# Reordering the loads of an attention stage: which wait the loads of one cycle stand behind

## The chip, the cores and the metric

The kernel runs on one core of a Trainium2 chip, as one program. The time is the device time of one execution in microseconds (us); the median of several executions counts. One further execution is taken by the hardware profiler, and its trace is read in the profile: engine by engine, instruction by instruction. TensorE (PE, with its weight loads PEld) does the matmuls, VectorE (DVE) and ScalarE (ACT) work on the results, GpSimd (POOL) helps, and SyncE (SP) issues nearly all DMA transfers, strictly in the order of its own list of instructions.

## The reference

One layer of a hybrid encoder, with 2048 tokens on a grid of 32 x 64, 1024 channels and 16 heads of 64: RMS norm, one projection into queries, keys, values and gates, neighbourhood attention in two dimensions, a SiLU gate, the output projection with the residual, and a final RMS norm.

```python
h = rmsnorm(x, g)
q, k, v, gate = jnp.split(h @ w_in, 4, axis=-1)
# each query sees 8 rows x 16 columns of keys around it, with a learned bias per head and offset
s = jnp.where(col_valid, einsum(qr, kr) * scale + bias, NEG_INF)
o = einsum(softmax(s), vr)
x = x + (o * jax.nn.silu(gate)) @ w_out
return rmsnorm(x, norm_f)
```

## The kernel before

Everything is computed in float32 accuracy; large products run as three products of halves of the mantissa, with a split of each operand into a high and a low part (ScalarE copies, VectorE subtracts).

`stage_one` (L617) and `stage_two` (L1011) compute most of the projections, by a seven-product scheme, and write queries, keys, gates and values to DRAM (`qd`, `kd`, `sgd`, `vd`). Then comes the attention stage, which this change is about: the loop at L1825 to L1880 with 32 cycles and one more to end it. A cycle is one pair of heads `p` and one quarter `T` of the tokens, in the order of `order` (L1221). In program order cycle `m` is:

- `begin(m)` (L1804): makes a list of loads, which the clock then issues;
- `feed(...)`: matmuls of 512 columns that fill the time, from the projections that are still missing (`projections`, L1197) and later from the output product of the first rows (`outputs`, L1564); between them VectorE, ScalarE and GpSimd normalise the scores of the cycle before;
- `turns(m - 1)` (L1358): 48 transposes of the normalised scores, with copies by ScalarE and VectorE (L1376, L1378);
- `scores(2m)`, `scores(2m + 1)` (L1310): 64 matmuls of queries and keys, then bias and exponent (L1332, L1340);
- `values(m - 1)` (L1382): 36 matmuls of scores and values, and one product with the gate (L1399). The result, attention's output, is stored to DRAM by `keep` (L1402).

So on TensorE a cycle of about 9 us is: filling matmuls, transposes, scores, values, and again.

The order of the work is laid out by a planner that runs when the program is built. `clock[0]` counts the filling matmuls, and `now()` (L273) adds 26 for each cycle that is over. `store(key, lag, f)` (L330) puts an action into the list `later`, due `lag` matmuls from now, and `due` (L336) carries it out when the clock gets there; `later_loads` (L1796) does so for a list of loads, 0.5 apart. `all_loads` (L1800) issues those that are left when the next cycle begins.

What cycle `m` loads by `begin`, in this order: the gate of cycle m - 1 (`load_sg`, L1260), the two bias tables of cycle m + 1 (`load_bias`, L1268), its queries (`load_q`, L1243) and keys (`load_k`, L1226), and the values of cycle m (`load_v`, L1252). All are issued by SyncE. A load waits until the buffer that it overwrites is free. There are two buffers for queries, so the queries of cycle m + 1 wait for the scores of cycle m - 1 (the last before `begin(m)`); two for values, so those of cycle m wait for `values(m - 2)`. Gates have two buffers, tables ten, keys one for even and one for odd pairs of heads; these are free early. Because SyncE keeps its order, whatever stands behind the queries in the list waits for the same scores, and whatever stands behind the values waits for the values section. Keys of `T` = 0 and 3 add only four rows (128 KB) to those of the quarter before.

The second kind of loads: weight blocks. `items` (L261) lists what the fillers still need: blocks of `w_in`, four blocks of x, blocks of `w_out`. `load_ahead` (L293) keeps five of them loaded ahead of their use, and `load_item` (L154) issues the load at once, at the place of the program where the planner happens to be. `consume` (L300) uses the next block, which means the split by ScalarE and VectorE (L185, L186, L190, L191). In the attention stage it does so only in a `turn`, or when a product can't go on without it (`asked`), and only when the block was asked for at least 36 units of `now()` ago.

Of the kernel before, what the change touches and what calls it, by code (L numbers as in the profile page):

```python
# [61 lines left out]
def build(ctx, tc, x, xr, xt, wg, bias, w_out, n0, nf, out):  # L62
# [87 lines left out]
    raws, wh, wl, asked_at = {}, {}, {}, {}  # L150
# [3 lines left out]
    def load_item(it):  # L154
        kind, a, b = it
        t = raws[it] = raw([128, 512], F32, "raw")
        asked_at[it] = now()
        if kind == "x":
            nc.sync.dma_start(t, xt[a * 128:(a + 1) * 128, b * 512:(b + 1) * 512])
        elif kind == "w":  # L160
            nc.sync.dma_start(t, wg[a[0], :, 512 * b:512 * b + 512])
        else:
            nc.sync.dma_start(t, w_out[a * 128:(a + 1) * 128, b * 512:(b + 1) * 512])

    def use_item(it):
        kind, a, b = it
        state["event"] = clock[0]
        t = raws.pop(it)
        if kind == "x":
            normed("x%d1" % (a // 4 + 1), b, a % 4, t)  # L170
            split_to(hh[a, b], hl[a, b], t, None)
        elif kind == "w":
            u, ph = a
            if KINDS["v"] <= u < KINDS["g"]:
                t = t.rearrange("p (k c) -> p k c", c=256)
                a = u // 2 * 2, ph
                if u % 2 == 0:
                    wh[a, b] = wp([128, 2, 512], F32R, "wh")
                    wl[a, b] = wp([128, 2, 512], F32R, "wl")
                s = slice(u % 2 * 256, u % 2 * 256 + 256)  # L180
                h, l = wh[a, b][:, :, s], wl[a, b][:, :, s]
            else:
                w = wp([128, 2, 512], F32R, "w")
                wh[a, b], wl[a, b] = h, l = w[:, 0], w[:, 1]
            nc.scalar.activation(h, t, AF.Copy)  # L185
            nc.vector.tensor_tensor(l, t, h.bitcast(F32), OP.subtract)  # L186
        else:
            h, l = xs([128, 512], F32R, "woh"), xs([128, 512], F32R, "wol")
            woh[a, b], wol[a, b] = h, l
            nc.scalar.activation(h, t, AF.Copy)  # L190
            nc.vector.tensor_tensor(l, t, h.bitcast(F32), OP.subtract)  # L191
# [62 lines left out]
    attending = [False]  # L254
# [6 lines left out]
    items, seen = [], set()  # L261
# [11 lines left out]
    def now():  # L273
        return clock[0] + 26 * runs[0]

    freed = set()
    state = dict(used=0, loaded=0, half=-1, done_halves=0, event=0.0)

    def may_use(it):
        kind, a, b = it  # L280
        d = state["done_halves"]
        if kind == "w":
            def tiles_(a, b):
                return (a[0] // 2 * 2, a[1], b) if KINDS["v"] <= a[0] < KINDS["g"] else (*a, b)
            live = {tiles_(*i[1:]) for i in items[:state["used"]] if i[0] == "w" and last_use["w", i[1]] >= d} - freed
            return sum(1 + (KINDS["v"] <= t[0] < KINDS["g"]) for t in live | {tiles_(a, b)}) <= 8
        if kind == "x":
            return sum(last_use["x", i] >= d for i in {i[2] for i in items[:state["used"]] if i[0] == "x"} - {b}) < 2
        if kind == "o":
            return last_use["x", 2 + b] < d  # L290
        return True

    def load_ahead():  # L293
        while state["loaded"] < min(len(items), state["used"] + AHEAD):
            load_item(items[state["loaded"]])
            state["loaded"] += 1

    quiet = [False]

    def consume(n, asked=False, turn=False):  # L300
        for _ in range(n):
            load_ahead()
            if attending[0] and not asked and not turn:
                return
            if state["used"] == len(items) or not may_use(items[state["used"]]):
                return
            if attending[0] and now() - asked_at[items[state["used"]]] < 36 and not asked:
                return
            it = items[state["used"]]
            state["used"] += 1  # L310
            use_item(it)

    def need(it):
        while it in items[state["used"]:]:
            before = state["used"]
            consume(1, True)
            assert state["used"] > before, (it, items[state["used"]])
# [25 lines left out]
    def must(*keys):  # L343
        assert all(k in written for k in keys), keys
        for n in range(len(later) - 1, -1, -1):
            if later[n][1] in keys:
                for _ in range(n + 1):
                    later.pop(0)[2]()
                break
# [871 lines left out]
    order = [(p, T) for p in range(NP) for T in (1, 0)] + [(p, T) for p in range(NP - 2) for T in (2, 3)]  # L1221
# [4 lines left out]
    def load_k(p, T):  # L1226
        r0, r1, more = PARTS[T]
        base = 12 * (T > 1)
        a, b = r0 * GW, r1 * GW + more
        must(*[("k", p, c) for c in range(a // 512, (b + 511) // 512)])  # L1230

        def keys():
            if T in (1, 2):
                khalf.clear()
                KT[p, T // 2] = (kp([128, 2048], F32, "kt") if p % 2 == 0 else mkp([128, 1536], F32, "kt"))[:, :1344]
            t = KT[p, T // 2]
            if T == 2:
                nc.gpsimd.memset(t[:, 1280:1288], 0.0)
            nc.sync.dma_start(t[:, a - base * GW:b - base * GW], kd[p][:, a:b])

        return keys

    def load_q(p, T):  # L1243
        must(("q", p, T))

        def queries():
            QT[p, T] = qp([128, 512], F32, "q")
            nc.sync.dma_start(QT[p, T], qd[p][T])

        return queries  # L1250

    def load_v(p, T):  # L1252
        r0, r1 = FRAME[T], FRAME[T] + TALL
        must(*[("v", p // 4, t) for t in range(r0 // 2, (r1 + 1) // 2)])
        rows = vd[p // 4][p % 4][r0 * 8192:r1 * 8192].rearrange("(k x) -> k x", x=1024)
        t = vp([128, 1024], F32, "vt")
        VT[p, T] = t.rearrange("p (s d) -> p s d", s=8)
        nc.sync.dma_start(t[:8 * TALL], rows)

    def load_sg(p, T):  # L1260
        must(("g", p, T))
        SG[p, T] = sp([128, 512], F32, "sgt")
        nc.sync.dma_start(SG[p, T], sgd[p][T])
# [4 lines left out]
    def load_bias(p, T):  # L1268
        fs = []
        kind = BRINGS[T]  # L1270
        w = 2 * WIDE * TABLES[kind][2]
        EM[p, T // 2, kind] = []
        for quad in range(2):
            t = mp([128, 512], F32, "em")[:, :w]
            EM[p, T // 2, kind].append([t[:, :w // 2], t[:, w // 2:]])
            o = TABLE_AT[kind] + quad * w
            fs.append(lambda t=t, o=o, w=w: nc.sync.dma_start(t, bias[p, 128 * o:128 * (o + w)].rearrange("(q c) -> q c", c=w)))
        return fs
# [372 lines left out]
    def load_rows_of(m, f, home=None):  # L1651
        n, half = PAIRS[m][int(f[1]) - 1], int(f[2]) - 1
        T, i = divmod(n, 4)
        must(*[("og", p, T) for p in range(NP) if p // 4 == half])
        A[m, f] = (home or raw)([128, 512], F32, "raw")
        nc.sync.dma_start(A[m, f].rearrange("p (k q) -> p k q", k=4), ogd[T][i, half])
# [139 lines left out]
    def later_loads(fs, lag, step):  # L1796
        for k, f in enumerate(fs):
            store(("load",), lag + k * step, f)

    def all_loads():  # L1800
        while any(e[1][0] == "load" for e in later):
            later.pop(0)[2]()

    def begin(m):  # L1804
        all_loads()
        quiet[0] = False
        fs = [lambda: load_sg(*order[m - 1])] if m else []
        if m + 1 < cycles:
            nx = order[m + 1]
            fs += load_bias(*nx)  # L1810
            fs += [load_q(*nx), load_k(*nx)]
        if m < cycles:
            fs.append(lambda: load_v(*order[m]))
        later_loads(fs, 0.5, 0.5)
        if m == cycles - 1:
            later_loads([land_first], 1.5, 0)
            later_loads([lambda f=f, i=i: load_rows_of(i, f) for i in ((2, 0, 1) if PLAIN <= 6 else (0, 1)) for f in ("A11", "A12")], 10, 0.5)
        if m == cycles:
            later_loads([land_rest], 4, 0)
# [5 lines left out]
    for m in range(cycles + 1):  # L1825
        a = amount[m] - 8
        begin(m)
        feed(HALF_HEAD)
        if m:
# [88 lines left out]
```

## Time and profile before

| | |
|---|---|
| median of 3 runs | 993.05 us (992.84 to 994.57) |
| the profiled execution | 993.25 us, of which the span from first to last instruction is 991.5 us |
| granted TensorE clock | 0.999 |
| TensorE busy | 979.3 us, 99% of the span |
| VectorE, ScalarE, GpSimd busy | 76%, 54%, 16% |
| attention stage | about 560 to 870 us of the span |
| DMA in the span | 227.93 MB, mean 230 GB/s |

In the profile, L12 is line 12 of the kernel. A group of matmuls is written as its line, its output and inputs by the program's names, shapes and count. "Idle before" is time in which the engine had nothing running; behind the arrow stands what ended it, and "issue" means that the profile shows no semaphore, so no engine and no transfer, on which it waited. A matmul's end is modelled: matmuls overlap, and a short stop hides in part behind the modelled end of the matmul before. In the attention stage `q`, `kt`, `vt`, `sgt` and `em` are the loads of queries, keys, values, gate and tables, `ogd` the store of attention's output, and `raw` a weight block. A DMA's row in the timeline shows when SyncE issued it and how long issuing took; the time to landing is counted from the start of the issue.

### The profile page before, as it was taken

Reading aid. Unit: us, or ns where it says so; the run is one execution under the profiler, and the core shown is the slowest. Engines: PE = TensorE matmul, PEld = TensorE weight load, DVE = VectorE, ACT = ScalarE, POOL = GpSimd, SP = SyncE. Lnnn points to the kernel's source line nnn. Section 1 sums busy time; section 2 is a strip of 40 time slices with the busy share of each in tenths; the row PEclk is TensorE's granted clock in tenths of the full one; section 3 lists DMA queues with packets and bytes.
Section 4 is the critical chain, followed back from the end, with each engine's and each line's share of the span. In section 5 each row is a group of like instructions: output and inputs, shape, how many; then the busy total and the mean of one; then the engine's idle time right before and its main releaser. Section 6 shows DMA issues by size and latency. Waiting matters only on the chain.

```text
span 991.5 us, 22624 instructions
## 1 busy us (share of the span) xinstructions
PE 979.3 (99%) x8172; PEld 797.0 (80%) x8172; DVE 755.2 (76%) x1735; ACT 531.5 (54%) x1310; POOL 159.6 (16%) x430
## 2 busy tenths in 40 slices
PE   9999999999999999999999999999999999999997
PEld 7888888888888888888888778777778777888886
DVE  6899888988665876766775677668778878877866
ACT  7773245455535342343433467677777776654443
POOL 0000001231100000000001133333343332302110
PEclk9999999999999999999999999999999999999999
DMA  8943547777957836657565799878989978697754
GB/s 287 337 130 102 196 132 256 248 242 251 368 159 225 276 116 201 189 182 224 169 176 203 247 302 271 264 226 279 307 277 288 298 222 266 223 379 212 205 146 117
DMA packets 149968, 227.93 MB, mean 230 GB/s; under 512 B 13536, under 2 KB 66016, under 8 KB 149856
## 3 DMA queue, kind: packets, MB, share of 16 engines
q1 hardware_dynamic: 146832, 221.37, 70.2%
q0 software_dynamic: 2592, 4.72, 2.8%
q8 instruction: 64, 1.05, 0.4%
q14 instruction: 48, 0.39, 0.1%
q10 hardware_dynamic: 432, 0.40, 0.1%
HBM read 160.37 MB, written 66.06 MB: 228 GB/s over the span
## 4 chain that ended last, share of the span: by engine, by line
PE 99%; issue 1%; DVE 0%; ACT 0%
PE pp L446 40%; PE pv L612 13%; PE py L1695 12%; PE o L1395 8%; PE s L1323 6%; PE ph L1372 5%; PE pp L388 2%; PE pp L384 2%; PE pp L386 2%; PE pv L727 2%; PE po L1600 2%; PE po L1604 2%; PE po L1602 2%; PE zp L127 0%; PE prb L235 0%
## 5 line engine op out<-in xcount | busy, mean ns | idle before, releaser
L446 PE MATMUL pp<-h,f 128*128 128x512 f32 x576 | 185.3, 389 | 0.0
L446 PE MATMUL pp<-t,f 128*128 128x512 f32 x702 | 171.4, 389 | 0.0
L446 PEld LDWEIGHTS pp<-t,f 128*128 128x128 f32 x702 | 131.8, 188 | 27.4
L1340 ACT ACTIVATE x<-sums,st 128x264 f32<-128x264 f32 (+1 forms) x256 | 124.5, 488 | 30.0 <-DVE st L1332 30.0
L446 PEld LDWEIGHTS pp<-h,f 128*128 128x128 f32 x576 | 108.1, 188 | 22.6
L446 PE MATMUL pp<-l,f 128*128 128x512 f32 x288 | 112.0, 389 | 0.0
L1352 POOL TENSOR_SCALAR x<-x,st 128x264 f32<-128x264 f32 (+1 forms) x192 | 88.5, 477 | 113.7 <-DVE st L1347 93.8
L1332 DVE CUSTOM_DVE_ANT_0 sums<-s,em 128x253 f32<-128x253 f32 (+1 forms) x256 | 91.1, 401 | 6.2 <-ACT x L1340 1.7
L429 DVE TENSOR_TENSOR f<-raw,f 128x512 fp32r<-128x512 f32 x105 | 75.9, 727 | 19.4 <-ACT f L428 19.3
L1395 PE MATMUL o<-pta,vt 120*64 120x192 f32 (+2 forms) x1152 | 85.1, 300 | 4.0 <-issue 4.0
L1395 PEld LDWEIGHTS o<-pta,vt 120*64 120x64 f32 x1152 | 70.2, 137 | 23.2 <-issue 16.4
L428 ACT ACTIVATE f<-raw 128x512 fp32r<-128x512 f32 x105 | 63.4, 622 | 36.6 <-DVE raw L435 22.0
L1376 DVE COPY pta<-ph 120x512 f32<-120x512 f32 x96 | 60.3, 684 | 18.3 <-PE ph L1372 18.1
L1378 ACT ACTIVATE pta<-ph 120x512 f32<-120x512 f32 x96 | 50.4, 599 | 37.8 <-PE ph L1372 37.8
L446 PEld LDWEIGHTS pp<-l,f 128*128 128x128 f32 x288 | 54.0, 188 | 11.3
L1323 PE MATMUL s<-kt,q 64*32 64x253 f32 (+1 forms) x2048 | 59.2, 362 | 0.7 <-issue 0.7
L1372 PEld LDWEIGHTS ph<-ident,x 64*120 64x120 f32 x1536 | 47.6, 135 | 11.3 <-issue 10.6
L612 PE MATMUL pv<-wh,t 128*128 128x512 f32 x176 | 56.2, 389 | 0.0
L1695 PE MATMUL py<-woh,f 128*128 128x512 f32 x168 | 55.4, 390 | 0.0
L467 POOL TENSOR_TENSOR tmp<-tmp,rb 128x512 f32<-128x512 f32 x18 | 28.5, 1582 | 157.6 <-DVE tmp L464 137.2
L446 PE MATMUL pp<-sixths,f 128*128 128x512 f32 x198 | 52.7, 389 | 0.0
L1372 PE MATMUL ph<-ident,x 64*120 64x64 f32 x1536 | 52.0, 221 | 0.0
(231 smaller groups left out, 1889.4 us busy)
## 6 DMA issues: line engine op xcount, KB each, us to landing
raw<-in_wg_dram SPq DMA_DIRECT2D x124, 256.0 KB, 4.8
vt<-vd SPq DMA_DIRECT2D x32, 480.0 KB, 5.2
row<-in_xr_dram SPq DMA_DIRECT2D x32, 256.0 KB, 5.2
vd<-v SPq DMA_DIRECT2D x32, 256.0 KB, 3.2
sgd<-sg SPq DMA_DIRECT2D x32, 256.0 KB, 3.8
q<-qd SPq DMA_DIRECT2D x32, 256.0 KB, 3.6
sgt<-sgd SPq DMA_DIRECT2D x32, 256.0 KB, 5.3
ogd<-og SPq DMA_DIRECT2D x32, 256.0 KB, 5.3
```

Source lines behind the costliest of these rows:

```text
L428: nc.scalar.activation(t[:, 0], src, AF.Copy)
L429: nc.vector.tensor_tensor(t[:, 1], src, t[:, 0].bitcast(F32), OP.subtract)
L446: nc.tensor.matmul(B[n, P], t[:, int(m == 2), c], x[k][int(m == 1)], start=P in (1, 6, 5) and k == 0 and m == 0, stop=k == 3 and m == 2, s ...
L612: nc.tensor.matmul(p, a[:, o], b, start=P in (1, 6, 5) and k == 0 and m == 0, stop=k == 3 and m == 2, skip_group_check=True)
L1323: nc.tensor.matmul(places[half, s][h * 32:h * 32 + 32], qt[a, g * 64 + half * 32:g * 64 + half * 32 + 32], kt[a, o:o + n * GW].rearrange(" ...
L1332: nc.vector.tensor_tensor_reduce(rows[s][:, :, :WIDE], places[half, s].rearrange("p (r c) -> p r c", c=WIDE), table[s].rearrange("p (r c) ...
L1340: nc.scalar.activation(to, rows[s].rearrange("p r (b c) -> p b r c", b=3), AF.Exp, bias=st[:, o:o + 1], scale=-1.0, accum_out=st[:, 4 + o: ...
L1352: nc.gpsimd.tensor_scalar(t, t, f, 1.0, op0=OP.mult, op1=OP.mult)
L1372: nc.tensor.transpose(ph[h][:k, o:o + 64], X[quad, half, s][q, at:at + k], ident[q, q])
L1376: nc.vector.tensor_copy(o, i_)
L1395: nc.tensor.matmul(o[s * 64:s * 64 + 64, g0 * 64:g1 * 64], vt[:k, strip, s * 64:s * 64 + 64], moving, start=strip == 0, stop=strip == 7, s ...
L1695: nc.tensor.matmul(B[m, P], t[:, a, c], b, start=P in (1, 6, 5) and k == 0 and i == 0, stop=k == 3 and i == 2, skip_group_check=True)
```

## The change

Two things change. In the attention stage a weight block that the planner asks for is no longer loaded at that place; it is put on a list `asked`, and the list is loaded as one entry of begin's list, or at once when a product can't go on without a block. The age at which a block may be used becomes 30 units of `now()` from its load instead of 36, and a block that is not yet loaded counts as of age 0. Second, begin's list is reordered: queries, keys, asked weight blocks, gate, tables, values, where it was gate, tables, queries, keys, values.

```diff
+    asked = []
+
+    def load_asked():
+        while asked:
+            load_item(asked.pop(0))
+
     def load_ahead():
         while state["loaded"] < min(len(items), state["used"] + AHEAD):
-            load_item(items[state["loaded"]])
+            asked.append(items[state["loaded"]])
             state["loaded"] += 1
+        if not attending[0]:
+            load_asked()
 
-    def consume(n, asked=False, turn=False):
+    def consume(n, needed=False, turn=False):
         for _ in range(n):
             load_ahead()
-            if attending[0] and not asked and not turn:
+            if attending[0] and not needed and not turn:
                 return
             if state["used"] == len(items) or not may_use(items[state["used"]]):
                 return
-            if attending[0] and now() - asked_at[items[state["used"]]] < 36 and not asked:
+            if needed and items[state["used"]] in asked:
+                load_asked()
+            if attending[0] and now() - asked_at.get(items[state["used"]], now()) < 30 and not needed:
                 return
...
     def begin(m):
         all_loads()
         quiet[0] = False
-        fs = [lambda: load_sg(*order[m - 1])] if m else []
+        fs = [load_asked]
+        if m:
+            fs.append(lambda: load_sg(*order[m - 1]))
         if m + 1 < cycles:
             nx = order[m + 1]
-            fs += load_bias(*nx)
-            fs += [load_q(*nx), load_k(*nx)]
+            fs = [load_q(*nx), load_k(*nx)] + fs + load_bias(*nx)
         if m < cycles:
             fs.append(lambda: load_v(*order[m]))
         later_loads(fs, 0.5, 0.5)
```

## The prediction

> **What bounds the kernel now.** I read the page first: TensorE is busy for 99% of the span, so a reordering of loads can only take away, or add, moments in which it stands still.
>
> ```profile
> PE 979.3 (99%) x8172; PEld 797.0 (80%) x8172; DVE 755.2 (76%) x1735; ACT 531.5 (54%) x1310; POOL 159.6 (16%) x430
> q8 instruction: 64, 1.05, 0.4%
> ```
>
> The profiled execution took 993.25 us, its span 991.5, so 1.75 us lie around the span; the median of the runs is 993.05, 0.2 lower. The second row is the one that later matters: 64 packets of 1.05 MB together, about 16 KB each, on a queue of kind "instruction". TensorE has 2 x 8172 instructions; 1.05 MB over them is 64 bytes apiece. I take this queue for the one that brings TensorE its own program, one packet for about 127 matmuls and their weight loads.
>
> Next the waits, for TensorE alone, and, in the stretch of attention (560 to 872 us), the line in which another engine waits for a weight block.
>
> ```profile
> PE o L1395 <- issue: 4.0, 4, 2.1
> PE s L1323 <- issue: 0.7, 1, 0.7
> DVE w L186 <- DMA raw<-in_wg_dram: 0.7, 1, 0.7
> ```
>
> TensorE never waits for a load of queries, keys, values, gates or tables. Its five stops, 4.8 us (2.06 + 0.35 + 0.74 + 0.88 + 0.74 in the rows below), wait for "issue", for nothing that the profile names. The timeline of TensorE shows them, below a cycle without one (644.78).
>
> ```profile
> 644.78 2.62 PE L1395 MATMUL o<-pta,vt 120*64 120x128 f32 x36
> 647.33 0.50 PE L386 MATMUL pp<-l,w 128*128 128x512 f32 x1
> ...
> 586.48 2.07 PE L1395 MATMUL o<-pta,vt 120*64 120x128 f32 x28
> 590.61 0.77 PE L1395 MATMUL o<-pta,vt 120*64 120x192 f32 x8 [2.06 <-issue]
> 591.30 0.50 PE L388 MATMUL pp<-h,w 128*128 128x512 f32 x1
> ...
> 626.60 2.06 PE L1395 MATMUL o<-pta,vt 120*64 120x192 f32 x23 [0.35 <-issue]
> ...
> 663.41 0.61 PE L1323 MATMUL s<-kt,q 64*32 64x253 f32 x2 [0.74 <-issue]
> ...
> 729.29 2.56 PE L1395 MATMUL o<-pta,vt 120*64 120x128 f32 x34 [0.88 <-issue]
> ...
> 795.07 2.34 PE L1395 MATMUL o<-pta,vt 120*64 120x128 f32 x30 [0.74 <-issue]
> ```
>
> A values section takes 2.55 us (644.78 to 647.33); the one at 586.48 takes 4.82, 2.27 more, of which the profile calls 2.06 idle, because a matmul's modelled end hides part of a stop. So the five cost between 4.8 and, at some 0.4 hidden in each, 6.8 us: an estimate of 6.5, which is all that this change could win. Counting matmuls from the span's start to each stop, with the view of busy time by windows, tells what they are:
>
> ```profile
> 0.00:588.24 588.24, 587.04 (x2869) 1.00 0.68 216
> 0.00:625.93 625.93, 622.68 (x3500) 1.00 0.70 220
> 0.00:662.30 662.30, 658.71 (x4131) 1.00 0.71 223
> 0.00:728.13 728.13, 723.80 (x5266) 1.00 0.72 226
> 0.00:794.07 794.07, 788.85 (x6402) 1.00 0.74 232
> ```
>
> The differences are 631, 631, 1135 and 1136 matmuls: 5, 5, 9 and 9 times 126.2. TensorE stops only where one packet of its program ends and the next has not come. The DMA view of 0.2 us pieces finds those packets: one begins between 661.0 and 661.2 and one between 726.8 and 727.0, each 2.2 to 2.5 us before TensorE goes on (663.41, 729.29).
>
> ```profile
> q8 instruction: 1, 0.02, 30.5%
> q8 instruction: 1, 0.02, 32.3%
> ```
>
> The Trainium skill (Runtime: NRT & Kernel Launch, Instruction fetch mechanics) says the same of the size, a refill in 16 KiB blocks, and calls the cost of a block boundary mostly hidden; by that the stops would be something else and the change worth nothing, but the five boundaries in this trace are not hidden.
>
> **What holds the packet up.** The timeline of the DMA queue of SyncE over one cycle, and the time to landing of two of the values' loads (issued 655.90 and 721.49):
>
> ```profile
> 649.13 0.46 SPq L1263 DMA_DIRECT2D sgt<-sgd  x1
> 649.64 1.53 SPq L1277 DMA_DIRECT2D em<-in_bias_dram  x2
> 653.44 0.33 SPq L1248 DMA_DIRECT2D q<-qd  x1
> 653.81 0.43 SPq L1239 DMA_DIRECT2D kt<-kd  x1
> 655.90 0.34 SPq L1258 DMA_DIRECT2D vt<-vd  x1
> 656.63 0.38 SPq L1402 DMA_DIRECT2D ogd<-og  x1
> ...
> DMA to landing us min/median/max: 4.5/4.5/4.5
> ...
> 721.49 0.34 SPq L1258 DMA_DIRECT2D vt<-vd  x1
> 722.22 0.38 SPq L1402 DMA_DIRECT2D ogd<-og  x1
> ...
> DMA to landing us min/median/max: 5.4/5.4/5.4
> ```
>
> The values landed at 660.4 and 726.9; the packets of code began at 661.0 to 661.2 and 726.8 to 727.0. So a packet asked for about when the values section ends starts only when the values' load, issued just before, is done. In the second case the store of attention's output, 0.73 us behind the values' load, did not hold it up, so the request fell into that gap.
>
> **The change, part by part.** Of begin's list, gate and tables (649.13, 649.64) go behind queries and keys, so behind the end of a scores section. *Queries and keys* stand behind that end already, by the first row below: no gain, 0.
>
> ```profile
> SPq L1248 <- PE s L1323: 66.9, 25, 5.4
> SPq L1258 <- PE o L1395: 46.9, 29, 7.2
> vt<-vd SPq DMA_DIRECT2D x32, 480.0 KB, 5.2
> sgt<-sgd SPq DMA_DIRECT2D x32, 256.0 KB, 5.3
> em<-in_bias_dram SPq DMA_DIRECT2D x32, 184.0 KB, 5.2
> raw<-in_w_out_dram SPq DMA_DIRECT2D x16, 256.0 KB, 5.0
> ```
>
> *Gate*: 5.2 us later (649.13 to about 654.3, right behind the keys' issue); with 5.3 to landing it is there at 659.6, and L1399 reads it only behind the values section that follows the scores at 663.41: 0, with about 6 us of cover. Were it gone, each microsecond would hold VectorE and then a PSUM bank. *Tables*: 5.2 us later too, needed one scores section later than the one at 663.41: 0. *Weight blocks*: a block is no longer loaded when its predecessor is used but at the next begin, and used after at least 30 instead of 36 of the planner's units. A cycle adds 26 and about 13.5 units, so a block asked for in one cycle is issued in the next and used in one after that, as before; ScalarE's and VectorE's work keeps its order: 0. Cover: no line above shows ScalarE waiting for a block; if a use came too early it would wait up to the 5.0 us of the last row. *Values* keep their wait for the values section (second row) but stand behind three more issues (0.46 for the gate, 1.0 to 1.5 for two tables, by twice the gate's and by the 1.53 of the row) and sometimes a weight block, about as long as the gate. SyncE is then free 1.5 to 2.5 us after 654.3, when TensorE leaves the values section at 655.8: the values' issue slips by 0 to 1 us; they are read a cycle later, so that alone costs 0. Stores behind them slip alike, also 0. Begin issues nothing on ScalarE's or GpSimd's queue, and TensorE's own instructions stay the same and in the same order.
>
> What remains is the packet of code. Ahead of the values' load now stand, in the same cycle, the gate and two tables: at least 624 KB (256 + 2 x 184). At the 321 GB/s of a busy stretch (below) that is 2.0 us. Against it: these loads were issued before, too, only in front of the queries, and what counts is how much idle DMA time their later start throws away.
>
> ```profile
> 653.50:654.50 1.00, 1.00 (x21) 0.93 (x19) 1.00 (x9) 1.00 (x6) 0.00 (x0) 1.00 0.54 123
> 656.00:657.50 1.50, 1.50 (x7) 1.21 (x7) 1.06 (x4) 1.27 (x5) 1.49 (x4) 1.00 0.23 52
> 657.50:661.50 4.00, 4.00 (x88) 3.19 (x94) 2.52 (x5) 2.40 (x5) 0.62 (x5) 1.00 0.98 321
> ```
>
> In this cycle 0.46 + 1.16 = 1.6 us of DMA time lay idle between queries and values, and the moved 2.0 us fall into them: the values land some 0.4 later. Bounds for one stop: +2.0 (no idle time in front), and minus the whole stop (the packet gets in front of the values). I take +0.3, nearest to the cycle that has rows. Five stops: +1.5 us, so 993.25 + 1.5 = 994.75, and with the 0.2 between profile and median, 994.6.
>
> **Rivals.** *Faster: the packet slips past the values' load.* The values' issue comes up to 1 us later, and the request fell less than 0.73 us behind it. If SyncE's five or six issues in a row delay the values by more than about 0.7 us, the packet waits for the tables alone. The values would then come behind it, 480 KB or 1.5 us at 321 GB/s and their own slip of 0.7, so the packet starts some 2 us sooner; that would end the four short stops (0.35 + 0.74 + 0.88 + 0.74 = 2.7 idle, about 4 with what is hidden) and leave the first: 989.0. For it: two tables took up to 1.53 us to issue. Against it: singly the issues sum to no more than the values section lasts.
>
> *Slower: one unbroken batch.* If the DMA engines have no idle time between scores and values (0.98 in the last row), each stop grows by the 2.0 us less what little idle remains, say 1.2, and boundaries that now just pass become stops of about 0.5 (between the first and the last stop lie 28, of which five stopped; I allow one more): 5 x 1.2 + 0.5 = +6.5, and 999.5 beside the median. It decides from the point where the values land more than 1 us later behind the queries' issue than the 7.0 us of the rows (653.44 to 660.4).
>
> *Nothing: the packet does not stand behind loads.* Then the stops stay as they are: 993.1. By the Trainium skill (DMA: Bandwidth & Descriptors, Queues, rings and completion order) each DMA engine takes turns between its queues packet by packet, so a packet of code would hardly wait for what SyncE has queued. The trace speaks against that: 661.0 and 726.9 both follow the values' landing. That the change does not do what it says belongs here too: the loads move, and TensorE does not notice.
>
> **How the numbers follow.** A difference of 0.2%, 2 us, is what a measurement of this kernel can tell from none. Forecast 0.40, its own range 992.3 to 997.0 (a quarter of it past +2 us); faster rival 0.24; slower rival 0.25; nothing 0.11. Faster: 0.24 and 0.03 of the forecast's lower edge, 0.27. Slower: 0.25 and 0.10 from the forecast, 0.35. Same: 0.38. The range reaches to the values of the two rivals, 989.0 to 999.5; what lies beyond them is the farther half of either, about 2 in 10.
>
> **What would show it.** Right: in the timeline, queries, keys, a weight block, gate and tables in one run behind each scores section, then values and the output's store; matmul counts of 8172; stops again multiples of 126.2 matmuls apart, each 2.3 us behind an instruction packet, and that packet behind the landing of values; the sum of "issue" waits on TensorE up by about 1.5 us. Wrong: a wait of ScalarE at L190 or VectorE at L1399 for a load; stops gone or doubled; packets of code that start in the middle of the values' load.

## The result, and the profile after

| | before | after |
|---|---|---|
| median, same chip, in turns | 992.94 us (990.84 to 994.97, 12 runs) | 999.04 us (995.25 to 1008.12, 12 runs) |
| ratio, 95% interval | | 1.0068 (1.0041 to 1.0094) |
| the profiled execution, its span | 993.25, 991.5 us | 998.88, 996.8 us |
| granted TensorE clock | 0.999 | 0.999 |

The change costs 0.7%, about 6 us: above the 994.6 that was forecast, just inside the range's upper end of 999.5. From the page of after, the rows that answer to those of before (in part 6: KB of one load and median us from issue to landing):

```profile
PE 980.8 (98%) x8172; PEld 797.5 (80%) x8172; DVE 755.3 (76%) x1735; ACT 532.1 (53%) x1310; POOL 159.1 (16%) x430
q8 instruction: 64, 1.05, 0.4%
...
vt<-vd SPq DMA_DIRECT2D x32, 480.0 KB, 7.0
...
sgt<-sgd SPq DMA_DIRECT2D x32, 256.0 KB, 5.2
```

TensorE does the same 8172 matmuls and is busy 1.5 us longer; the span grew by 5.3, so most of the loss is standing still. It is lost in the attention stage: from its 2600th to its 7600th matmul TensorE takes 290.6 us in before and 294.9 in after (288.0 and 300.1 in a second profile of each, below), and behind that, to the end of the span, 125.4 to 126.0 us in all four. The values land 7.0 us after their issue instead of 5.2 (medians). TensorE's waits, of after:

```profile
PE o L1405 <- issue: 6.9, 6, 1.8
...
PE pv L737 <- ACT h L557: 1.1, 1, 1.1
PE s L1333 <- issue: 0.7, 1, 0.7
```

The waits that name no engine and no transfer went from 4.7 us in five to 7.6 in seven. (The 1.1 us at L737 is in stage one, which the change doesn't touch; the second profile of this kernel, below, has none there.) The timeline of TensorE shows the seven:

```profile
590.86 0.76 PE L1405 MATMUL o<-pta,vt 120*64 120x192 f32 x8 [1.23 <-issue]
...
628.47 0.70 PE L1405 MATMUL o<-pta,vt 120*64 120x192 f32 x6 [1.44 <-issue]
...
658.25 0.43 PE L1405 MATMUL o<-pta,vt 120*64 120x128 f32 x2 [0.51 <-issue]
...
666.17 0.61 PE L1333 MATMUL s<-kt,q 64*32 64x253 f32 x2 [0.67 <-issue]
...
732.92 0.88 PE L1405 MATMUL o<-pta,vt 120*64 120x128 f32 x13 [1.78 <-issue]
...
799.53 0.99 PE L1405 MATMUL o<-pta,vt 120*64 120x128 f32 x13 [1.56 <-issue]
...
828.95 0.77 PE L1405 MATMUL o<-pta,vt 120*64 120x192 f32 x8 [0.38 <-issue]
```

The view of busy time by windows counts the matmuls up to each of them (x behind PE):

```profile
0.00:590.80 590.80, 587.35 (x2869) 482.20 (x2869) 446.22 (x757) 276.48 (x547) 43.23 (x64) 1.00 0.68 215
0.00:628.40 628.40, 623.52 (x3500) 510.48 (x3500) 473.89 (x859) 302.78 (x629) 56.00 (x110) 1.00 0.70 218
0.00:658.20 658.20, 652.80 (x4005) 533.81 (x4005) 493.44 (x937) 323.43 (x696) 67.30 (x150) 1.00 0.71 221
0.00:666.10 666.10, 660.04 (x4131) 539.17 (x4131) 498.74 (x952) 327.62 (x706) 69.11 (x156) 1.00 0.71 220
```

2869, 3500 and 4131 are the counts of before, to the matmul (the view is cut just ahead of each stop); so are the next two, 5266 and 6402. The stops are at the same ends of packets of TensorE's program, three of the five longer, one as before, one (590.86) shorter. New are 4005, one packet ahead of 4131, and the one at 828.95. Counted from the start of one matmul to the start of the next, less the usual distance, the stops of before sum to 6.3 us and those of after to 9.7. That is how stops are counted from here on. Over all profiles of this document there are 86 of them, and each ends 2.2 to 2.8 us after a packet of code begins.

Now one stop close by, the one that grew from 0.88 to 1.78 us idle, at 5266 matmuls. SyncE's queue of after, from the end of the scores:

```profile
721.77 0.32 SPq L1258 DMA_DIRECT2D q<-qd  x1
722.14 1.13 SPq L1249 DMA_DIRECT2D kt<-kd  x1
723.32 0.42 SPq L163 DMA_DIRECT2D raw<-in_w_out_dram  x1
723.79 0.43 SPq L1273 DMA_DIRECT2D sgt<-sgd  x1
724.26 0.91 SPq L1287 DMA_DIRECT2D em<-in_bias_dram  x2
725.27 0.68 SPq L1268 DMA_DIRECT2D vt<-vd  x1
726.04 0.49 SPq L1412 DMA_DIRECT2D ogd<-og  x1
```

One run, without a pause of SyncE, as the diff says. By the view of the tiles, the gate issued at 723.79 took 6.8 us to land (730.6), and the values issued at 725.27 took 8.3 (733.5):

```profile
DMA to landing us min/median/max: 6.8/6.8/6.8
...
DMA to landing us min/median/max: 8.3/8.3/8.3
```

The DMA view of 730.2 to 730.4 holds the packet of code, 2.6 us before TensorE goes on at 732.92:

```profile
q8 instruction: 1, 0.02, 41.3%
```

So this packet did get in front of the values; it began as the gate had all but landed, with the tables still on their way. In before the packet at the same place began at 726.8 to 727.0, behind values that had been issued right after queries and keys:

```profile
719.03 0.33 SPq L1248 DMA_DIRECT2D q<-qd  x1
719.40 0.67 SPq L1239 DMA_DIRECT2D kt<-kd  x1
721.49 0.34 SPq L1258 DMA_DIRECT2D vt<-vd  x1
```

From the issue of the queries to the packet it is 7.9 us in before (719.03 to 726.9) and 8.5 in after (721.77 to 730.3). By the Trainium skill (DMA: Bandwidth & Descriptors, Queues, rings and completion order) a DMA engine takes turns between its queues. That agrees with a packet that passes the values and the tables; that it began only 5.9 us after the packet before it was entered at 724.5 is not what that section would lead one to expect.

The new stop at 658.25 shows the other side. Its packet began between 655.7 and 655.9; the values issued at 649.99 took, by the view of the tiles of after,

```profile
DMA to landing us min/median/max: 6.4/6.4/6.4
```

and landed at 656.3. In before the same packet began between 652.6 and 652.8, and the values issued at 647.44 took

```profile
DMA to landing us min/median/max: 5.7/5.7/5.7
```

and landed at 653.1. Each time the packet starts some 0.5 us ahead of the values' landing, so it doesn't wait for that landing, also in before. TensorE had entered the packet ahead of it at 650.6 in before and at 652.5 in after; behind that the values' landing moved from 2.5 to 3.8 us and the packet from 2.1 to 3.3, and with that the 4.8 to 5 us of work in between no longer hid the fetch. That the two moved together is what these rows show; which of them moved the other they don't.

SyncE's waits of after show the order from another side:

```profile
SPq L1258 <- PE s L1333: 113.8, 28, 6.9
...
SPq L1268 <- PE o L1405: 9.8, 5, 6.6
...
SPq L1439 <- DMA ogd<-og: 7.6, 1, 7.6
```

The values waited for a values section 29 times in before, 46.9 us; now 5 times, 9.8 us. Mostly SyncE reaches them only when the section has ended: here it ended at 724.1, and they were issued 1.1 us later. Over the 30 cycles the values are issued 0.1 to 2.6 us behind the end of a values section, in 13 of them over 1 us; in before it is 0.1 us in all but one. The last row is a load that reads attention's output back (`ograw`): SyncE waited 4.8 us in before for the store `ogd` to land, and waits 7.6 us here, where the store stands at the end of the longer run.

### The profile page after: what moved, and what is told of

It reads as the page before. It is cut to its first block, busy times and chain, and to the rows that moved or that the text cites. A ratio compares the mean times of both kernels' runs of the same rounds, so it can differ in the third digit from the quotient of the medians.

```text
span 996.8 us, 22621 instructions
## 1 busy us (share of the span) xinstructions
PE 980.8 (98%) x8172; PEld 797.5 (80%) x8172; DVE 755.3 (76%) x1735; ACT 532.1 (53%) x1310; POOL 159.1 (16%) x430
## 4 chain that ended last, share of the span: by engine, by line
PE 98%; issue 1%; DMA 1%; SPq 0%; ACT 0%; DVE 0%
PE pp L456 40%; PE pv L622 13%; PE py L1705 11%; PE o L1405 8%; PE s L1333 6%; PE ph L1382 5%; PE pp L398 2%; PE pp L394 2%; PE pp L396 2%; PE pv L737 2%; PE po L1614 2%; PE po L1610 2%; PE po L1612 2%; DMA land<-in_xt_dram 1%; SPq L567 0%
## 5 line engine op out<-in xcount | busy, mean ns | idle before, releaser
L1382 PEld LDWEIGHTS ph<-ident,x 64*120 64x120 f32 x1536 | 47.6, 135 | 11.3 <-issue 10.6
```

The costliest lines, as they stand in the source:

```text
L1382: nc.tensor.transpose(ph[h][:k, o:o + 64], X[quad, half, s][q, at:at + k], ident[q, q])
```

## The experiments

A ratio is to runs of the kernel before on the same chip. "Stops" are those at ends of packets in the attention stage of the one profiled execution, "late" the packets, of 39 there, that begin over 3 us after TensorE enters the packet before, "half clock" the time with a granted clock of 0.5, the last 5 us of the span left out. A count of late packets is good to about one, since some begin near 3 us. The profiled execution can lie well off its kernel's median: 1001.25 us for extra load, 1003.59 for after again and 993.87 for before, half a packet.

| kernel | median us | ratio (95%) | span us | stops us (number) | late | half clock us |
|---|---|---|---|---|---|---|
| before, first profile | 992.94 | | 991.5 | 6.3 (5) | 11 | 0 |
| before, again | 991.18 | 0.9993 (0.9979 to 1.0006) | 989.3 | 3.7 (4) | 9 | 0 |
| after, first profile | 999.04 | 1.0068 (1.0041 to 1.0094) | 996.8 | 9.7 (7) | 18 | 0 |
| after, again | 999.95 | 1.0084 (1.0055 to 1.0113) | 1001.8 | 11.5 (8) | 17 | 6.8 |
| order alone | 998.91 | 1.0063 (1.0039 to 1.0086) | 998.3 | 10.6 (8) | 17 | 3.4 |
| blocks alone | 995.27 | 1.0027 (1.0010 to 1.0045) | 993.5 | 7.2 (5) | 11 | 0 |
| values behind output | 998.21 | 1.0064 (1.0039 to 1.0089) | 996.0 | 10.0 (8) | 18 | 0 |
| extra load | 997.44 | 1.0044 (1.0023 to 1.0066) | 999.3 | 10.1 (6) | 21 | 3.4 |
| nine more matmuls | 994.37 | 1.0019 (1.0002 to 1.0035) | 991.6 | 4.2 (4) | 8 | 0 |
| after, tables once | 995.45 | 1.0032 (1.0012 to 1.0051) | 991.6 | 6.3 (4) | 12 | 0 |
| before, tables once | 989.83 | 0.9973 (0.9958 to 0.9988) | 988.8 | 2.4 (3) | 6 | 0 |
| values behind tables | 996.46 | 1.0034 (1.0019 to 1.0049) | 994.7 | 4.1 (5) | 9 | 3.4 |
| values behind keys | 1000.09 | 1.0068 (1.0045 to 1.0091) | 998.0 | 0.6 (1) | 13 | 6.8 |
| values behind tables, last early | 992.43 | 1.0003 (0.9988 to 1.0018) | 988.8 | 1.0 (2) | 12 | 0 |
| after, values first | 994.00 | 1.0031 (1.0015 to 1.0046) | 991.8 | 5.2 (5) | 14 | 0 |
| after, half a packet | 999.98 | 1.0077 (1.0063 to 1.0092) | 998.2 | 7.0 (6) | 17 | 3.4 |
| before, half a packet | 990.14 | 0.9988 (0.9977 to 0.9999) | 992.1 | 3.8 (3) | 13 | 3.4 |
| both | 991.57 | 0.9995 (0.9983 to 1.0007) | 989.3 | 2.0 (2) | 14 | 0 |

**Which half of the change.** Order alone takes the new list of `begin` and leaves the weight blocks as they were; blocks alone does the reverse.

```diff
-            fs += load_bias(*nx)
-            fs += [load_q(*nx), load_k(*nx)]
+            fs = [load_q(*nx), load_k(*nx)] + fs + load_bias(*nx)
```

> Begin's list in the new order, weight blocks still loaded where the planner asks for them. If TensorE's packets of code wait behind what SyncE queued ahead of the values' load, this part carries the loss: 3 to 6 us slower than before, stops on 'issue' summing to 9 or more against 6.5. If the deferred weight blocks are the cause: within 1 us of before.

> Weight blocks deferred to begin's list (behind keys, ahead of values) and the age of 30, but gate and tables ahead of the queries as before. Queue theory: only in the cycles with a block is the values' load pushed back, by 0.8 us a block: 0 to 1.5 us slower than before. If the deferred blocks are the cause of the loss: 4 to 6 us slower.

The order alone has the whole loss, 1.0063 where the whole change has 1.0068. Deferring the blocks costs something by itself, 1.0027, but adds nothing that can be seen to the order. Waits of TensorE, order alone:

```profile
PE o L1395 <- issue: 8.1, 7, 2.1
...
PE s L1323 <- issue: 0.4, 1, 0.4
```

8.5 us against 4.7: the same kind of wait, at the line numbers of before.

**Are they packets?** Nine more of the zero matmuls that open the program: packets then begin nine matmuls earlier in the work.

```diff
-    for _ in range(8):
+    for _ in range(17):
         nc.tensor.matmul(zp, z[:, :128], z, start=True, stop=True)
```

> The kernel before with 17 instead of 8 matmuls of zeros at its start, where TensorE waits for its first operands: the rest of its program moves by 18 instructions against the packets of code, and nothing else changes. Theory of the packets: stops stand again where one packet ends, at counts of matmuls and weight loads that are the same multiples of 126.2 matmuls from the start (2869, 3500, 4131, ...), though other matmuls stand there now; which boundaries stop changes, and the time moves by at most 4 us either way. If a stop belonged to a place of the program (its semaphores, its banks): the same matmuls stop as before, at counts 9 higher, and the time stays within 1 us.

Matmuls up to three of its stops:

```profile
0.00:591.00 591.00, 588.37 (x2869) 482.50 (x2869) 446.54 (x757) 275.97 (x546) 42.82 (x63) 1.00 0.68 216
0.00:663.50 663.50, 660.80 (x4131) 539.69 (x4131) 498.39 (x950) 326.79 (x704) 69.07 (x156) 1.00 0.70 222
0.00:786.90 786.90, 783.12 (x6277) 637.12 (x6277) 597.54 (x1312) 423.51 (x1008) 115.94 (x323) 1.00 0.73 232
```

The counts stay, 2869 and 4131, though the work at these counts now stands nine matmuls earlier in the program: a stop belongs to a packet and not to a place in the attention. The third is one packet ahead of 6402 (125). The Trainium skill (Runtime: NRT & Kernel Launch, Instruction fetch mechanics) calls such a boundary mostly hidden; here 31 or more of 39 are, and the rest cost 0.6 to 11.5 us.

**The values' load, moved in the kernel before.** First behind the store of attention's output, then into the list of the next cycle, behind the tables or behind the keys:

```diff
-            fs.append(lambda: load_v(*order[m]))
+            later_loads([lambda: load_v(*order[m])], 4.5, 0)
```

> The kernel before, but the values' load stands behind the store of attention's output, so it is issued some 0.7 to 1.1 us later. Queue theory: packets of code asked for at the end of a values section get in front of the 480 KB of values, stops shrink: 1 to 4 us faster than before, and the packets in question start more than 1 us earlier after the values section. If packets do not stand behind loads, or if the stop is set elsewhere: within 1 us of before.

```diff
             fs += load_bias(*nx)
+        if m:
+            fs.append(lambda: load_v(*order[m - 1]))
+        if m + 1 < cycles:
             fs += [load_q(*nx), load_k(*nx)]
-        if m < cycles:
-            fs.append(lambda: load_v(*order[m]))
```

> The kernel before, but a cycle's values are loaded a little later, in the list of the next cycle behind gate and tables: issued some 2.7 us after the values section instead of 0.1, and the packet of code that is asked for there meets the output's store and the gate alone. Queue theory: stops at the end of a packet that is asked for near a values section shrink from about 6 us in all to 2 to 3, so 2 to 5 us faster than before. If the 1.3 us of the run with values behind the output's store show the rule, that later values only move the stops to other boundaries: within 2 us, or slower by up to 6.

(The next has the two new lines behind the queries and keys.)

> The kernel before, but a cycle's values are loaded in the next cycle's list behind queries and keys, so they wait for a scores section and no longer for a values section: issued 2.5 us before a values section ends instead of 0.1 after it. Queue theory: 480 KB are through the queue 1.5 to 2.5 us earlier when the packet is asked for, stops shrink by about half: 1 to 4 us faster than before. If what counts is one large batch behind the scores, as in the changed kernel: 2 to 6 us slower.

The queue theory had forecast a gain for all three, and all three are slower. The first shows the theory's limit: a load that only moved past a 256 KB store, and so 1.2 us later behind the values section, goes with 18 late packets instead of 11 or 9, and costs 0.6% in all. Output, values, gate and tables follow one another there in one run, but so do values, output, gate and tables in before. The second has stops of 4.1 us, no more than before has (6.3 and 3.7); what it lost is elsewhere:

```profile
PE o L1395 <- DMA vt<-vd: 3.0, 1, 3.0
PE o L1395 <- issue: 2.2, 3, 1.0
```

The last cycle has no scores ahead of its values section, so the last values come 3.0 us too late, and behind that wait the clock is at half for 3.4 us. In the third kernel the last values come 4.6 us too late, the clock is at half for 6.8 us from within that wait on, and another 1.2 us of waiting for `vt` and 2.5 for VectorE come earlier. Put right for the last cycle, with all else as in the second:

```diff
-        if m:
+        if 0 < m < cycles:
             fs.append(lambda: load_v(*order[m - 1]))
...
+        if m == cycles - 1:
+            fs.append(lambda: load_v(*order[m]))
```

> Values one cycle later, between tables and queries, as in the run that put them behind the tables, but the last cycle's values where the kernel before has them. In that run's profile the stops at packet boundaries in attention came to 4.1 us against 6.3 before, and attention's last transposes began at 865.3 against 866.8 us; the loss came behind it, 3.0 us of waiting for the last values and a clock of 0.5 for 3.4 us. Theory (a packet of code waits behind the data loads that SyncE has queued around the end of the values section): with the last values early both losses go, 3.0 + 1.7 us, so 996.5 - 4.7 = 991.8, 0 to 2 us below the kernel before, and no wait of TensorE for vt. Rival (the loads' place only moves stops about, and those of one profile are chance): no gain over before, 993 to 995, though the wait for vt is gone.

The wait and the half clock are gone, the stops are down to 1.0 us (a wait of 0.9 us for ScalarE has come), and the ratio is 1.0003 for 1.0034; but that is the kernel before, no better. Its profiled execution, 990.62, was one of its faster ones. The rival was right that nothing is gained.

**What stands in front.** More of it in the kernel before: 512 KB from DRAM to DRAM per cycle, ahead of the values.

```diff
             fs += [load_q(*nx), load_k(*nx)]
+            fs.append(lambda: nc.sync.dma_start(more[m], wg[m // 2, :, 1024 * (m % 2):1024 * (m % 2) + 1024]))
```

> The kernel before with 512 KB more from DRAM to DRAM in each cycle, behind the keys and ahead of the values; nobody reads them. Queue theory: values' landing and the packet behind it slip by 1.6 us or more in each cycle, the five stops grow by that and more boundaries become stops: 6 to 15 us slower, all of it 'issue' on TensorE at distances that are multiples of 126.2 matmuls. If packets take turns with the loads: within 2 us of before.

It is slower by 0.4%, 4 us rather than 6 to 15, and not within 2 us either: 21 packets are late, stops of 10.1 us. Less of it, first in after and then in before:

```diff
+        if p:
+            EM[p, T // 2, kind] = EM[0, T // 2, kind]
+            return []
```

> The changed kernel without the bias tables of the pairs of heads 1 to 7: all use those of pair 0, so that 368 or 506 KB in each cycle are not loaded (this leaves out part of the computation). Queue theory: what stands ahead of the packet in the changed order is the gate and the tables; without them the stops fall from about 9 us to 3 or less, 6 to 9 us faster than the changed kernel and 0 to 4 faster than before. If the loss has nothing to do with what stands in SyncE's queue: as slow as the changed kernel, 5 to 6 us over before.

> The kernel before, with the tables of pairs 1 to 7 not loaded and those of pair 0 used in their place (this leaves out part of the computation). Theory (what counts is what stands in the queue between scores and the end of the values section): in the kernel before the tables stand ahead of the queries and land before the values are issued, so leaving them out changes little: within 1.5 us of before. Rival (all traffic counts, wherever it stands): as much gained as by the same omission in the changed kernel, 3.6 us, so some 989.

Without tables the changed kernel has 12 late packets, 6.3 us of stops and a ratio of 1.0032, so half of its loss goes, 3.6 us rather than the 6 to 9 that the theory gave. But the kernel before gains as well, 0.9973, 2.5 us, though its tables stand ahead of the queries: my bound of 1.5 us was too small. So loads that do not stand in the same run count too. And between these two there is still 0.6%, 5.7 us by the medians (3.2 above, 2.5 below the kernel before): with or without tables the new order costs nearly the same. Then the changed kernel with the values out of the run, at the head of the next cycle's list:

```diff
+        if 0 < m < cycles:
+            fs.insert(0, lambda: load_v(*order[m - 1]))
-        if m < cycles:
+        if m == cycles - 1:
             fs.append(lambda: load_v(*order[m]))
```

> The changed kernel, with the values of cycle m - 1 at the head of begin's list, ahead of queries and keys, so nothing stands behind gate and tables (the last cycle's values stay where they were). Theory (the packet has slipped past the values' load and waits for the tables): the values were not what held it, so the stops stay, 8 to 11 us in sum, and the time is 997 to 1000. Rival (the values' load, which shares the engines with the packet, is what makes it late): stops of 3 to 6 us, 992 to 995.

```profile
PE o L1405 <- issue: 3.2, 4, 1.1
...
PE s L1333 <- issue: 0.7, 1, 0.7
```

3.9 us of waits where after has 7.6, and 994.0: more than half of the loss is gone. I had expected nothing, because the packet at 730.3 had passed the values; the rival's numbers hold, stops of 5.2 us and 994.0. With the values a cycle later in both orders (1.0031 here, 1.0003 in the kernel with the last values early) the new order costs 0.3% instead of 0.7 to 0.8. So of the loads in the run the tables matter little to the difference between the two orders, and the values much. By what way the values do it is argued and not shown: the packet at 5266 had passed them, and the new stop at 658.25 above is one that moved with their landing.

**Chance, or the few packets with least time.** After and before once more, then both with 63 small zero matmuls at the start, half a packet:

> The changed kernel once more, unchanged, for a second profile. Theory: stops at the same packet boundaries (22, 27, 31, 32, 41, 50 and 54 counted from the program's start; one more or fewer), 8 to 11 us in sum, and 997 to 1001 for the time. If which boundaries stop is chance, another set and another sum, and a time that differs from 999.0 by over 2 us.

> The kernel before, unchanged, for a second profile. If single profiles are to be trusted: stops at the same five packets (22, 27, 32, 41, 50; one more or fewer) and 5 to 8 us in sum. If chance decides: another set, and a sum outside of 4 to 9 us. Time within 0.2% of before either way.

```diff
         nc.tensor.matmul(zp, z[:, :128], z, start=True, stop=True)
+    for _ in range(63):
+        nc.tensor.matmul(zp[:, :64], z[:, :128], z[:, :64], start=True, stop=True)
```

> The changed kernel with 63 small zero matmuls more at the start (128x64 each, half a packet of 126.2 matmuls, some 2 to 4 us), so that every packet of code begins half a packet earlier in the work. Theory 1 (a denser run of loads makes packets late wherever they fall): it stays 4 to 9 us above the kernel before shifted in the same way, with 8 to 12 us of stops at other places of the cycles. Theory 2 (the order only happens to meet the packets with least time): stops of 2 to 7 us, as in the shifted kernel before, within 3 us of it.

> The kernel before with the same 63 small zero matmuls at the start. By both theories stops stand at other matmuls, 63 earlier in the work, and by packets at the same whole numbers or others. Time 2 to 4 us above the kernel before (the added matmuls) and -4 to +4 for the stops: 990 to 1000. It is the measure for the shifted changed kernel.

After stops again at six of its seven packets, and at two more; before at four of its five. The sums differ from profile to profile by some 2 to 3 us (9.7 and 11.5; 6.3 and 3.7, which by my bounds is the case of chance), so a single profile can't tell kernels that are 2 us apart. Half a packet on, the windows of before and after show other counts, and these agree with each other:

```profile
0.00:680.10 680.10, 678.28 (x4510) 555.08 (x4511) 512.61 (x1004) 341.43 (x750) 75.92 (x180) 1.00 0.71 223
0.00:710.60 710.60, 706.82 (x5015) 577.66 (x5016) 536.80 (x1096) 365.28 (x826) 87.53 (x222) 1.00 0.72 226
```

```profile
0.00:673.60 673.60, 671.54 (x4384) 550.06 (x4385) 506.59 (x988) 336.45 (x738) 73.83 (x173) 1.00 0.71 222
0.00:711.60 711.60, 707.73 (x5015) 578.39 (x5016) 536.43 (x1094) 364.71 (x823) 87.21 (x221) 1.00 0.71 224
```

The first fence is before, the second after, both shifted; 5015 less 4510 is four packets, less 4384 five. None of these packets stopped unshifted, and yet the changed kernel is again slower than the kernel before shifted alike, 999.98 against 990.14, by 9.8 us, with 17 late packets against 13. The time goes with Theory 1, and even beyond its 4 to 9 us; the stops, 7.0 us against 3.8, stay below its 8 to 12 and reach just the end of Theory 2's range. Part of the loss is of another kind here, in the shifted changed kernel:

```profile
SPq L1441 <- DMA ogd<-og: 9.0, 1, 9.0
...
737.70 1.15 ACT L1453 ACTIVATE gh<-ograw 128x512 fp32r<-128x512 f32 x2 [3.48 <-DMA ograw<-ogd]
...
739.39 3.02 PE L1335 MATMUL s<-kt,q 64*32 64x253 f32 x62 [1.78 <-ACT pta L1390]
```

SyncE waits 9.0 us for the store at the end of a run before it can read attention's output back (5.1 in the shifted kernel before), ScalarE waits 3.5 us for that load, its copies of the transposes come late, and TensorE stands for 1.8 us with no packet involved; 0.7 us behind that the clock is at half for 3.4 us. So the new order does not merely meet some unlucky packets: it makes packets late at other places too, and it makes a store late that a load waits for.

**Both.** Values behind the tables (the last early) and the shift put together:

> The kernel before with the values one cycle later behind the tables (the last cycle's early) and the 63 small zero matmuls at the start. If stops are what separates the kernels: 2 to 4 us of stops against 3.7 and 6.3 in the two profiles of the kernel before, less 1.7 us for the added matmuls: 988 to 991, 1 to 3 us below the kernel before. Rival (single profiles vary as much as these differ): 990.5 to 993, not to be told from the kernel before.

2.0 us of stops, and 0.9995: of the kernels that do all of the work none beats the kernel before by more than the 0.12% of the shift alone, whose interval all but reaches 1.

## Why the prediction was wrong

*What held.* TensorE's 8172 matmuls and the other engines' work are unchanged; ScalarE at L190 and VectorE at L1399 wait for no load; stops stand at whole packets, each 2.3 to 2.7 us behind an instruction packet; queries, keys, block, gate, tables and values are one run.

*The step that failed* is the count in "Five stops: +1.5 us": it prices the boundaries that already stopped and puts all others at nothing, without a reason. The price itself, "I take +0.3" for a stop, came out near: over the same five packets the stops grew by 1.9 us in the first profile (2.4, 0.7, 1.1, 1.2, 1.0 became 1.6, 1.8, 1.0, 2.0, 1.8), and in the second they came to 6.3 us, where before has 6.3 and 3.7. With single stops up by 1.1 and down by 0.8 us that is in part luck. What the sum had not was new stops: two packets that do not stop in before take 1.5 us in the first profile of after, and four take 5.2 us in the second, with 6.8 us at half clock beside them. The change was decided at all 39 packets, of which 18 and 17 come over 3 us late instead of 11 and 9. Lateness alone is not yet a loss, as "both" shows with 14 late packets and 2.0 us of stops; it costs where the packet ahead holds little work. In after a packet that begins 4.7 us late costs nothing where the one ahead of it holds 7.7 us of work (636.1), and one that begins 3.6 us late costs 1.6 us where it holds 4.7 (590.9).

*Two smaller terms* were too low. "[T]he values' issue slips by 0 to 1 us": it slips by up to 2.6, in 13 of 30 cycles by more than 1. "Stores behind them slip alike, also 0": the store of attention's output lands later, and in the shifted changed kernel the load that waits for it stops TensorE for 1.8 us. And "starts only when the values' load, issued just before, is done" was read from two packets; a third one in the same profile, at 652.7, begins 0.4 us ahead of the values' landing.

*The slower rival* gave the time, 999.5 against 999.04, and its condition was met: the values land 11.8 us behind the queries' issue at 721.77 (733.5), where it decided from 8.0. But its sum was right by luck: it had 6 us for the five stops, which grew by some 2, and 0.5 for "one more" boundary, where two and four came and the half clock with them. Of its mechanism the run is unbroken and stops grow, but the packet need not wait for the values.

*The faster rival* had its premise come true, the packet that passes the values, and yet it lost. It had put the packet 2 us earlier than in before; the rows give it 0.6 us later behind the queries' issue (8.5 for 7.9), and a weight block and the gate now stand where the values had stood.

*What the prediction did not have* is the clock. The order alone and after again show it at half for 3.4 and 6.8 us behind stops at ends of packets, after shifted for 3.4 us behind the wait for ScalarE; of 3.4 us at half clock 1.7 us of work are lost. It is not the new order's alone: before shifted has 3.4 us too. It goes with the spread of after from 995 to 1010 us: of its 21 runs the seven above 1001 us had a granted clock of 0.994 to 0.997, the five below 997 us one of 0.998 to 1.0.

*What stays open*: which loads a packet stands behind, and so by what way the order makes it late. Against the landing of the values issued ahead of it the packet begins 0.7 us later (661.1 for 660.4), at the same time (726.9), 0.4 and 0.5 us earlier (652.7, 655.8) and 3.2 us earlier (730.3 for 733.5); over all profiles the landing of the loads issued up to a fixed time around the entry of the packet before goes with the packet's start by a correlation of only 0.3 to 0.4. Nor is it explained why the same exchange, values behind the output's store, costs 0.6% in the order of before and goes with a gain of 0.4 to 0.5% in that of after.

## What to carry to other kernels

When TensorE is 99% busy and its last waits name nothing, count the matmuls between them: steps that are whole multiples of one number point to packets of its program, and the DMA view shows whether one begins shortly ahead of each stop. Then price a reordering at every packet, not at those that already stop, and at every load that waits for a store at the end of a run. A load that nobody waits for can still cost time, and two orders of equal bytes differed by 6 us here.

## What the runs showed of the hardware

A stop of about 2 us can halve the clock for what follows. After, second profile, the stop at 772.32; first TensorE's timeline, then the windows around it (granted clock third from the end):

```profile
768.34 1.66 PE L1333 MATMUL s<-kt,q 64*32 64x253 f32 x51
772.32 0.82 PE L1333 MATMUL s<-kt,q 64*32 64x184 f32 x13 [2.32 <-issue]
773.07 3.95 PE L1405 MATMUL o<-pta,vt 120*64 120x128 f32 x36
```

```profile
769.00:772.30 3.30, 1.00 (x35) 0.47 (x19) 1.71 (x9) 2.06 (x9) 0.00 (x0) 1.00 0.57 146
772.40:775.80 3.40, 3.40 (x37) 2.42 (x39) 1.45 (x10) 1.98 (x8) 1.50 (x4) 0.51 0.43 119
775.80:779.20 3.40, 3.40 (x26) 2.74 (x23) 1.44 (x5) 1.27 (x3) 1.26 (x3) 0.99 0.93 252
```

The values section behind the stop has a row of 3.95 us instead of 2.62. Counted from start to start, less 0.08 us for the matmul itself, twelve stops of TensorE in attention were longer than 2 us over all profiles, at ends of packets or not; eight brought the half clock (the shortest 2.07 us) and four did not (the longest 2.48), and no half clock came there without such a stop. The Trainium skill (TensorE: Matmul & The Clock Gate, HAM oscillation) asks for no idle gaps above about 3.4 us. The 3.4 us that the half clock lasts agree with its window; as a safe length of a gap 3.4 us is too much here, since gaps of 2.07 to 2.6 us had the same effect six times.
